# A one-word-per-row load of w1 moved from ScalarE's queue to SyncE's, between the first two x loads

## The chip, the cores and the metric

The kernel runs on one core of one Trainium2 chip. The metric is the device time of one execution in microseconds. Engines are named as in the profile: PE (TensorE matmuls), PEld (its weight loads), DVE (VectorE), ACT (ScalarE), POOL (GpSimd) and SP (SyncE). SyncE, ScalarE and GpSimd each have a DMA queue of their own; in the profile SyncE's transfers run on q1, ScalarE's on q10 and GpSimd's on q0.

## The reference

```python
# x: 16 x 256 x 512, w1: 512 x 4096, w2: 2048 x 512, all float32
h = x @ w1
gate, value = np.split(h, 2, axis=-1)
h = np.maximum(gate, 0) * value
return (h @ w2).astype(np.float32)
```

With the batch flattened x has 4096 rows.

## The kernel before

The kernel computes both products in float16 with a seven-product scheme for 2 x 2 blocks, so each pair of blocks needs seven matmul groups (P1 to P7) in place of eight, and sums of operands are made beforehand. Rows of x are worked in four sets of 1024; a set is two halves (A1, A2) of 512 rows. Hidden columns go in 16 blocks of 128. For each set a loop over the blocks makes the gated hidden values g (the class `Block`), and the second product (`mm2_stream`) of one set runs between the matmuls of the next. The order of all instructions on each engine is written out by hand: what the program issues first on an engine or a queue runs first there.

The start is special, since nothing is on the chip yet. In the order in which things are issued:

- VectorE clears a tile `warm`, and TensorE runs eight matmuls on it (`idle(NWARM)`, L177) whose results are not used.
- ScalarE's queue has one transfer, L172: `first`, a tile of 128 x 4 float32 into which one word of each of the 512 rows of w1 is loaded. A row of w1 is 4096 float32, so the words lie 16 KB apart. No instruction reads `first`. ScalarE's only other transfer is L335, one of the last stores of the output.
- SyncE's queue has the loads of the first set: two of x rows 0 to 511 into `xf` (L418, 256 rows each; the profile calls that buffer g_S, since `xf` lies in a tile of that name), two of w1 for hidden blocks 0 and 1 (L404, `fetch_wl(0, 0, 2)` the gate columns and `fetch_wl(0, 1, 2)` the value columns; the profile calls the buffer g), one of further x rows (L421), two of w1 for block 2 (L404), and one more of x (L424). SyncE's next transfer is L558, far later.
- GpSimd makes the identity matrices, waits with a small copy (L427) for the value columns of blocks 0 and 1, and then fetches the rest of w1 and w2 with a cast to float16 (L358, L362).
- TensorE transposes the x rows (`turn_pair`, L382) in two halves; ScalarE and VectorE copy them out of PSUM (L384). They also cast the loaded w1 to float16 (`cast_w`, L400), first of all the gate columns of block 0. Then come the first real matmuls (`Plain`, L255), which need the transposed x and the cast w1. Three blocks go in this plain way; the seven-product blocks (L205) follow.

The order of the start, in the code:

```python
idle(NWARM)
turn_pair(xo, 0, psw, "W")      # x rows 0 to 255
cast_w(0, 0)                    # gate columns of block 0
idle(NFILL)
turn_pair(xo, 2, psx, "X")      # x rows 256 to 511
whole[0].gates((0,))            # first real matmuls
```

The last stores go out at the end of `mm2_stream`: SyncE's L330 and L337, and L335 on ScalarE's queue.

Of the kernel before, what the change touches and what calls it, by code (L numbers as in the profile page):

```python
# [9 lines left out]
F32, F32R, F16 = dt.float32, dt.float32r, dt.float16  # L10
# [6 lines left out]
P = 128  # L17
# [12 lines left out]
@with_exitstack  # L30
def kernel(ctx: ExitStack, tc: tile.TileContext, x, w1, w2, out):

    nc = tc.nc
    x2 = x.flatten_outer_dims()
    out2 = out.flatten_outer_dims()  # L40
    flagpool = ctx.enter_context(tc.tile_pool(name="flagpool", bufs=1))
    flag = flagpool.tile([1, 1], dt.int32, name="flag")
    with ExitStack() as fast:
        unfit = fast_way(fast, tc, x2, w1, w2, out2, flag)
    with tc.If(unfit > 0, label="general"):
        with ExitStack() as general:
            general_way(general, tc, x2, w1, w2, out2)
# [52 lines left out]
def fast_way(ctx, tc, x2, w1, w2, out2, flag):  # L100

    nc = tc.nc
# [10 lines left out]
    wpool = ctx.enter_context(tc.tile_pool(name="wpool", bufs=1))  # L113
# [8 lines left out]
    w1_v = w1.rearrange("(e p) (g j) -> p e g j", p=P, g=2)  # L122
# [44 lines left out]
    nc.vector.memset(warm[:, 0, :HALF], 0.0)  # L167
    ident = {t: wpool.tile([P, P], t, name=f"ident{k}") for k, t in enumerate((F32, F16))}
    gate = wpool.tile([P, 1], F32, name="gate")

    first = wpool.tile([P, 4], F32, name="first")
    nc.scalar.dma_start(out=first[:128], in_=w1_v[:128, :, 0, 0])  # L172

    def idle(n):
        for _ in range(n):
# [14 lines left out]
    def look(t, at, of):  # L190
        sq = tmp.tile([P, 1024], F16, name="sq", tag="sq", bufs=1)
        sq = sq[:, :of] if len(t.shape) == 2 else sq[:, :of].rearrange("p (a b) -> p a b", a=t.shape[1])
        nc.scalar.activation(sq, t, SQUARE, scale=(P / of) ** 0.5, accum_out=st[:, at:at + 1])
# [208 lines left out]
    def fetch_wl(jb, g_, n=1):  # L402
        c, i = place[jb]
        nc.sync.dma_start(out=wl[c][:, :, g_, i * P:(i + n) * P], in_=w1_v[:, :, g_, jb * P:(jb + n) * P])  # L404
# [7 lines left out]
    def look_x(s, i):  # L412
        b = i // 2
        t = rows[s, b // 2][:, b % 2] if s else (xf, xh)[b // NB][:, b % NB]
        look(t[:, i % 2 * 256:i % 2 * 256 + 256], 4 * NB * s + i, 256)

    for b in (0, 2):
        nc.sync.dma_start(out=xf[:, b:b + 2], in_=x_v[0, :, b:b + 2])  # L418
    fetch_wl(0, 0, 2)
    fetch_wl(0, 1, 2)  # L420
    nc.sync.dma_start(out=xg[:, :2], in_=x_v[0, :, NB:NB + 2])  # L421
# [116 lines left out]
    for s in range(NS):  # L538
        if s:
            g, go = g_tiles()  # L540
        first = NPLAIN if s == 0 else 0
# [111 lines left out]
```

## Time and profile before

| | |
|---|---|
| median of 14 runs | 309.54 us (309.23 to 310.46) |
| the profiled execution: time | 309.09 us |
| its span in the profile | 307.3 us |
| PE busy in the span | 299.7 us (98%) |
| DVE, ACT, POOL busy | 219.3, 189.8, 139.9 us |
| granted clock of TensorE | 1.00 |
| issue of L172 (`first`) on ScalarE's queue | at 0.82 us, 476 ns; landed 4.2 us after |
| issues of L418 (x) on SyncE's queue | at 0.85 and 1.38 us; landed 4.4 and 5.0 us after |

Times in the profile count from the start of the span. An issue's duration is that of the issuing engine's instruction, not that of the transfer; a landing is when its semaphore told of it. The share of DMA in a window is the mean busy share of the core's 16 DMA engines; as it is counted by a packet's start, it can be over 1.

### The profile page before, as it was taken

To read this page: it belongs to the slowest core of one execution; us is meant where nothing else is said; L and a number is where in the kernel's file an instruction comes from. 1 tells how busy PE (TensorE), PEld (TensorE's weight loads), DVE (VectorE), ACT (ScalarE), POOL (GpSimd) and SP (SyncE) were. 2 spreads that over 40 slices of the span, in tenths; PEclk is the share of its full clock that TensorE was granted. 3 is DMA by queue.
4 is the path that set the end of the run, shared out by engine and by line. 5 is a ranking of instruction groups with operands and counts; after the bars stand their busy time and mean duration, and the time that the engine had idled before them with its cause. 6 is when DMAs were issued, how large, how long until landed. Compare 5 with 4: busy or idle time off the path is not lost.

```text
span 307.3 us, 5116 instructions
## 1 busy us (share of the span) xinstructions
PE 299.7 (98%) x1868; PEld 182.1 (59%) x1868; DVE 219.3 (71%) x346; ACT 189.8 (62%) x457; POOL 139.9 (46%) x127
## 2 busy tenths in 40 slices
PE   7999999999999999999999999999999999999994
PEld 3574444588844444488864444458884444448883
DVE  1798898896468888884338888885526888888401
ACT  2557776568577676737856767656857767673230
POOL 1749999810004438990002345994000433898000
PEclk9999999999999999999999999999999999999999
DMA  6999986989615740064130000037321100000223
GB/s 226 305 204 205 210 207 184 188 152 192 233 59 102 140 102 1 2 132 143 68 139 23 12 34 2 0 69 140 138 82 57 34 10 26 0 2 0 70 87 124
DMA packets 34410, 31.54 MB, mean 103 GB/s; under 512 B 14448, under 2 KB 28784, under 8 KB 34160
## 3 DMA queue, kind: packets, MB, share of 16 engines
q1 hardware_dynamic: 24608, 20.32, 22.0%
q0 software_dynamic: 9104, 10.75, 21.3%
q8 instruction: 15, 0.25, 0.3%
q10 hardware_dynamic: 672, 0.13, 0.2%
q14 instruction: 11, 0.09, 0.1%
HBM read 24.12 MB, written 11.53 MB: 116 GB/s over the span
## 4 chain that ended last, share of the span: by engine, by line
PE 95%; DMA 2%; ACT 0%; SPq 0%; issue 0%; ACTq 0%
PE Y L205 26%; PE X L205 17%; PE W L205 17%; PE Y L291 14%; PE X L291 9%; PE W L291 9%; DMA g<-in_w_dram 2%; PE W L255 2%; PE X L255 1%; PE Y L255 1%; SPq L418 0%; PE X L390 0%; ACT Y L212 0%; ACT wr L400 0%; ACT pv L333 0%
## 5 line engine op out<-in xcount | busy, mean ns | idle before, releaser
L280 POOL TENSOR_TENSOR g_S<-g 128x512 f16<-128x512 f16 (+1 forms) x46 | 58.2, 1294 | 126.1 <-DVE g L244 126.1
L205 PEld LDWEIGHTS <-wt 128*128 128x128 f16 x488 | 47.7, 98 | 55.8 <-issue 0.3
L205 PE MATMUL X<-x_A,wr 128*128 128x512 f16 x244 | 72.5, 379 | 0.1
L205 PE MATMUL Y<-x_S,wt 128*128 128x512 f16 x244 | 72.6, 379 | 0.0
L205 PEld LDWEIGHTS <-wr 128*128 128x128 f16 x366 | 35.8, 98 | 41.4 <-issue 0.4
L232 DVE SCALAR_TENSOR_TENSOR cc<-W,pu 128x512 f32<-128x512 f32 x61 | 42.2, 692 | 24.1 <-ACT pu L226 24.1
L212 ACT COPY Y<-X 128x512 f32<-128x512 f32 x61 | 34.8, 570 | 38.0 <-PE X L205 37.5
L291 PEld LDWEIGHTS <-g_S 128*128 128x128 f16 x512 | 50.1, 98 | 5.8
L238 DVE SCALAR_TENSOR_TENSOR cc<-Y,pu 128x512 f32<-128x512 f32 x61 | 42.2, 692 | 6.2
L226 ACT ACTIVATE pu<-Y 128x512 f32<-128x512 f32 x61 | 36.4, 596 | 13.8 <-PE Y L205 13.8
L233 DVE SCALAR_TENSOR_TENSOR g<-X,cc 128x512 f16<-128x512 f32 x61 | 42.2, 692 | 2.4
L244 DVE SCALAR_TENSOR_TENSOR g<-Y,cc 128x512 f16<-128x512 f32 x61 | 41.6, 681 | 1.8 <-PE Y L205 1.8
L291 PEld LDWEIGHTS <-g 128*128 128x128 f16 x384 | 37.5, 98 | 8.2
L219 ACT ACTIVATE pu<-W 128x512 f32<-128x512 f32 x61 | 36.7, 602 | 0.3 <-PE W L205 0.3
L205 PE MATMUL Y<-x_A,wt 128*128 128x512 f16 x122 | 36.3, 379 | 0.0
L205 PE MATMUL W<-x_S,wt 128*128 128x512 f16 x122 | 36.3, 379 | 0.0
L205 PE MATMUL W<-x_S,wr 128*128 128x512 f16 x122 | 36.3, 379 | 0.0
L291 PE MATMUL X<-w,g 128*128 128x256 f16 x256 | 31.2, 273 | 0.0
L291 PE MATMUL Y<-v,g_S 128*128 128x256 f16 x256 | 30.6, 273 | 0.0
L321 DVE SCALAR_TENSOR_TENSOR o<-W,pv 128x256 f32<-128x256 f32 x16 | 6.8, 424 | 29.5 <-PE W L291 29.5
L280 POOL TENSOR_TENSOR g_S<-g,g_S 128x512 f16<-128x512 f16 x18 | 21.8, 1210 | 1.4
L280 POOL TENSOR_TENSOR g_S<-g_S,g 128x512 f16<-128x512 f16 x18 | 20.8, 1157 | 1.4
(76 smaller groups left out, 284.4 us busy)
## 6 DMA issues: line engine op xcount, KB each, us to landing
out_dram<-pv SPq DMA_DIRECT2D x15, 256.0 KB, 2.0
out_dram<-o SPq DMA_DIRECT2D x13, 256.0 KB, 2.4
x<-in_x_dram POOLq DMA_DIRECT2D x3, 1024.0 KB, 9.4
xn<-x SPq DMA_DIRECT2D x12, 256.0 KB, 3.0
g_S<-in_x_dram SPq DMA_DIRECT2D x4, 512.0 KB, 6.4
wr<-in_w_dram POOLq DMA_DIRECT2D x4, 512.0 KB, 13.0
w<-in_w_dram POOLq DMA_DIRECT2D x4, 512.0 KB, 15.3
g<-in_w_dram SPq DMA_DIRECT2D x2, 512.0 KB, 6.5
```

Source lines behind the costliest of these rows:

```text
L205: nc.tensor.matmul(ps, W(wn, self.jb)[:, b], self.xo[xn][:, b, :], start=fresh and b == 0, stop=b == 1, skip_group_check=True)
L212: nc.scalar.copy(out=self.Y, in_=self.X)
L219: nc.scalar.activation(self.p5, self.W, COPY, scale=GS)
L226: nc.scalar.activation(self.u2, self.Y, COPY, scale=-GS)
L232: nc.vector.scalar_tensor_tensor(out=self.c12, in0=self.W, scalar=GS, in1=self.u2, op0=MULT, op1=ADD)
L233: nc.vector.scalar_tensor_tensor(out=self.g[:, self.jb, :TH], in0=self.X, scalar=0.0, in1=self.c12, op0=MAX, op1=MULT)
L238: nc.vector.scalar_tensor_tensor(out=self.c22, in0=self.Y, scalar=-GS, in1=self.p5, op0=MULT, op1=ADD)
L244: nc.vector.scalar_tensor_tensor(out=self.g[:, self.jb, TH:], in0=self.Y, scalar=0.0, in1=self.c22, op0=MAX, op1=MULT)
L255: nc.tensor.matmul(ps[:, ts], W(names[e // 2], self.jb)[:, e % 2], self.a[:, e, ts], start=e == 0, stop=e == 3, skip_group_check=True)
L280: eng.tensor_tensor(go[n][:, h0:h1], go[i0][:, h0:h1], go[i1][:, h0:h1], op=op)
L291: nc.tensor.matmul(ps, go[gn][:, k, b * P:(b + 1) * P], V[vn][:, k, :], start=fresh and k == 0, stop=k == NHC - 1, skip_group_check=True)
L321: nc.vector.scalar_tensor_tensor(out=d["o1"][:, HALF:], in0=d["W"], scalar=1 / GS, in1=d["pu"][:, 1], op0=MULT, op1=ADD)
```

## The change

The load of `first` is taken from ScalarE's queue and issued on SyncE's, after the first of the two x loads and before the second. Its tile is allocated there too. Source words, destination shape and everything else stay as they are.

```diff
-    first = wpool.tile([P, 4], F32, name="first")
-    nc.scalar.dma_start(out=first[:128], in_=w1_v[:128, :, 0, 0])
-
...
+    first = wpool.tile([P, 4], F32, name="first")
     for b in (0, 2):
         nc.sync.dma_start(out=xf[:, b:b + 2], in_=x_v[0, :, b:b + 2])
+        if b == 0:
+            nc.sync.dma_start(out=first, in_=w1_v[:, :, 0, 0])
     fetch_wl(0, 0, 2)
     fetch_wl(0, 1, 2)
     nc.sync.dma_start(out=xg[:, :2], in_=x_v[0, :, NB:NB + 2])
```

SyncE's queue then has, in order: x rows 0 to 255, `first`, x rows 256 to 511, the two loads of w1 for blocks 0 and 1, and the rest as before. ScalarE's queue has L335 alone. On the other engines the instructions and their order are the same.

## The prediction

> **What bounds the kernel now.** I read the page's busy times first, then the chain of waits, then the timeline and the windows of the first microseconds, because all that the change touches happens there, and last the timeline of the end, where the only other transfer on ScalarE's queue sits.
>
> The page, engines and the chain that ended last:
>
> ```profile
> PE 299.7 (98%) x1868; PEld 182.1 (59%) x1868; DVE 219.3 (71%) x346; ACT 189.8 (62%) x457; POOL 139.9 (46%) x127
> ...
> PE 95%; DMA 2%; ACT 0%; SPq 0%; issue 0%; ACTq 0%
> ```
>
> TensorE sets the time, 95% of the chain, and the other 2% are one transfer. Which one, the chain in order of time says (start, length, what), window 0 to 13 us:
>
> ```profile
> 0.85 0.47 SPq L418
> ...
> 1.38 0.53 SPq L418
> ...
> 1.95 5.97 DMA g<-in_w_dram
> ...
> 7.95 0.41 ACT wr L400
> ...
> 8.40 1.10 PE X L255 x8
> 9.51 0.86 PE Y L255 x4
> ```
>
> SyncE issues the two x loads (L418, I call them x0 and x1), then the first w1 load (L404, the gate columns of hidden blocks 0 and 1). That one lands at 7.92, ScalarE casts it, and from 8.40 TensorE goes on to the end with hardly a pause. So the landing at 7.92 is the number to follow: what moves it moves the end by as much, since casts, Pool's fetches behind L427 and all later work hang on the same stream of landings.
>
> Issues, from the timeline (start, length, queue and line):
>
> ```profile
> 0.82 0.48 ACTq L172 DMA_DIRECT2D first<-in_w_dram  x1
> 0.85 1.05 SPq L418 DMA_DIRECT2D g_S<-in_x_dram  x2
> ...
> 1.32 1.28 ACT L384 ACT_TABLE_LOAD   x1 [1.32 <-PEq L637]
> ...
> 5.41 1.06 PE L382 MATMUL W<-ident,g_S 128*128 128x128 f32 x8 [0.87 <-DMA g_S<-in_x_dram]
> ...
> 303.30 0.38 ACTq L335 DMA_DIRECT2D out_dram<-pv  x1
> ```
>
> And the windows of those stretches; the columns that matter are the last two, the busy share of the DMA engines and GB/s:
>
> ```profile
> 2.00:2.45 0.45, 0.45 (x2) 0.15 (x1) 0.00 (x0) 0.45 (x1) 0.00 (x0) 1.00 0.35 38
> 2.45:2.95 0.50, 0.50 (x2) 0.15 (x1) 0.00 (x0) 0.16 (x1) 0.00 (x0) 1.00 0.03 0
> 2.95:3.25 0.30, 0.30 (x2) 0.15 (x1) 0.00 (x0) 0.00 (x0) 0.00 (x0) 1.00 0.56 198
> 3.25:5.70 2.45, 1.58 (x7) 0.62 (x6) 0.00 (x0) 0.00 (x0) 0.00 (x0) 1.00 1.06 391
> 5.70:7.10 1.40, 1.40 (x15) 1.24 (x13) 0.69 (x1) 0.59 (x1) 0.00 (x0) 1.00 1.09 360
> ```
>
> Small packets start near 2.0 (by the DMA queues' counts 242 of the 528 packets that ScalarE's queue has in the first 10 us lie between 2 and 3 us, and 9 of SyncE's), then for half a microsecond nothing moves on either queue, then x0, x1 and w1 run back to back on full engines. From about 3 us on the DMA engines are the bound of the start.
>
> **The change, part by part.**
>
> *ScalarE's queue loses L172.* Its issue took 0.48 us before the table load at 1.32. ScalarE then stands idle 3.9 us for the first transposes (the wait of L384 for PE W), so an earlier table load gains nothing.
>
> *SyncE's queue gets it, after x0.* A second x issue took 525 ns, `first` 476 ns, so x1 and every SyncE issue behind it (four L404, L421, L424) goes out some 0.48 us later, plus a gap of 0.06. Is that seen? x0 is 512 KB; at 391 GB/s that is 1.34 us, so it moves from about 2.95 to 4.4, x1 to 5.7, the first w1 load to 7.1 (estimates; the landing is seen at 7.92). x0 needed 2.1 us from issue (0.85) to bulk movement (2.95), the longest such lag here; x1, issued at 1.9 instead of 1.38, would be ready at 4.0, 0.4 before its turn, the w1 load at 2.5 + 2.1 = 4.6, a whole 1.1 early. So the later issue costs nothing, the cover being x0's own transfer; if that cover goes, it costs 0.48. Behind them SyncE comes to L558, which waits 35.5 us in all for w2, so nothing later notices. Pool's L427 waits 7.6 us for the second w1 load and its weight fetches are queued behind it: they move with the landings, not on their own.
>
> *Engine time of `first`.* The trace gives its queue 2.9% of the 16 engines in the first 10 us: 0.29 us per engine. Of this 0.16 (0.35 x 0.45) ran at 2.00 to 2.45, when no x was ready, and 0.13 between x0's packets. Behind x0 in one queue all 0.29 stands before x1 and the w1 load: **+0.16**.
>
> *The half microsecond without movement.* 2.45 to 2.95 has a DMA share of 0.03. The trace does not say whose it is. If it belongs to `first` (half of its rows asked for, their words not yet back), it moves with `first` to behind x0, where x1 waits for it in the same queue; if it belongs to whatever comes first on the engines, x0 now meets it, and `first` adds nothing. Bounds: minus 1.0 us (x0 starts at 1.95, where `first` started, instead of 2.95, and `first` passes smoothly) to plus 0.50 (x0 still starts at 2.95 and the pause appears a second time). I take **+0.50**: x0 was issued only 0.03 us after `first`, yet the 9 x packets that moved before the pause were followed by none until 2.95, so x has a slow first access of its own, and 4-byte reads of 512 far-apart rows are the likelier ones to have theirs.
>
> *ScalarE's last store.* L335 (303.30, lands 2.3 us later, 305.6, the last landing) becomes the first transfer on that queue. In this trace the first issue on ScalarE's queue took 476 ns, the second 377; SyncE's first issue 471 against 330 for its last. So **+0.10** on the path that ends last. To the first packet `first` took 1.18 (0.82 to 2.00) and L335's packets some 0.87: upper bound +0.10 + 0.31 = 0.41; lower bound 0.
>
> *Sum.* 0 + 0.16 + 0.50 + 0.10 = +0.76 us. The profiled execution took 309.09 (span 307.30 and 1.79 around it), which would become 309.85; the median of the 14 runs, 309.54, lies 0.45 above it and becomes 310.30.
>
> **Two rules of the Trainium skill against these rows.** The rows first: L172 lasted 0.82 to 1.30 and the first L418 0.85 to 1.32, side by side, and the first L418 (471 ns) was shorter than the second (525), which had no rival. "Perfetto Trace Analysis", section "DMA Instruction — HWDGE", says that one descriptor generator is shared by the issuing sequencers and locked for one at a time. By that rule x0 stood behind `first`, and the new order would free it: the sum would be the faster rival's below. The rows show no lock in the issue times; what happens after them they leave open. "DMA: Bandwidth & Descriptors", section "Issuing engines are not separate DMA queues", says that all issuing engines end on the same 16 DMA engines and that the choice of issuer only saves issue time; by it the sum is the hidden 0.48, so 309.54. The pause on both queues at once agrees with shared engines; but within one queue x1 has to follow `first`, which the rule leaves out.
>
> **Rivals.**
>
> *Faster: x0 no longer waits for `first`.* Mechanism: at the start both queues feed the same engines, `first` got its packets in at 2.00 and x0's bulk only at 2.95. With x0 ahead it may start at 1.95 and everything behind it up to 1.0 earlier: -1.0 + 0.16 + 0.10 = -0.74, 308.80. For it: the pause lies between `first`'s two halves, and both resume together. Against it: the 9 x packets that came through before the pause were stopped as well. It decides as soon as x0's lead exceeds 0.26. PE could use it: x0's transposes wait 0.87 us for x at 5.41, and the warming matmuls end at 4.54.
>
> *No change: the pause is the start's own.* x0 meets the same 2.95, and `first` passes behind it at the pace of its packets: +0.16 and 0 to 0.10, or an x0 earlier by one or two tenths: -0.1 to +0.3, 309.7 as the middle. For it: the second half of `first` went through between x0's packets with the engines at 1.06 busy, so its rows needed no visible wait once the engines were running. This is the strongest argument against my +0.50.
>
> *Much slower: the later issue shows as well.* If the engines run dry behind x0 because `first`'s 512 descriptors hold the queue, x1's 0.48 is no longer covered: 0.16 + 0.50 + 0.48 + up to 0.41 = +1.55, 311.1. Against it: the 1.1 us in hand of the w1 load.
>
> *The change does nothing.* `first` is never read by any instruction, so no wait is tied to it; only its place counts. That is the second rival with all terms at zero.
>
> **How the numbers follow.** A measurement of this kernel can tell about 0.2%, 0.6 us, from no change. Forecast (pause behind x0) 0.40; much slower 0.12; no change 0.24; faster 0.24. Of the forecast's 0.40 about 0.04 falls below +0.6, because part of the pause may be hidden under x0's last packets; of the faster case 0.02 stays within 0.6. So slower 0.36 + 0.12 = 0.48, same 0.24 + 0.04 + 0.02 = 0.30, faster 0.22. As the cases of both signs hold most of the chance: the forecast's own range is 309.9 to 310.7 (pause 0.1 to 0.5, tail 0 to 0.41). The range that should hold 8 in 10 reaches from the faster case's near half (308.9) to short of the much slower one (310.9).
>
> **What would show it.** In the profile after: the L404 landing now at 7.92 should come at about 8.6 and TensorE's first L255 at about 9.1; a stretch of low DMA share of up to 0.5 us should stand between x0 and x1 near 4.4 to 5; L418's second issue at 1.9; L335's issue near 0.48 us long. If instead x0's bulk starts before 2.6 the faster rival is right; if the landing is within 0.3 of 7.92 the pause is the start's own. If the landing is the same and the end later, it is ScalarE's queue. I am wrong altogether if TensorE shows new pauses after 10 us.

## The result, and the profile after

The changed kernel takes 312.07 us (median of 10 runs, 311.10 to 313.73), the kernel before 309.69 (47 runs): a ratio of 1.0078 [1.0066, 1.0091], 2.38 us slower. Two more executions of it, the profiled one among them, took 310.97 and 310.38 and are not in that median. A second measurement gave 311.88 against 309.88, 1.0053 [1.0031, 1.0075]. The forecast was +0.76 us. The sign is right; the size is a third of what came, and the time lies outside the range of 308.9 to 310.9.

The profiled execution took 310.97 us, with a span of 309.1 (before: 309.09 and 307.3). The lines between `first`'s old place and its new one have moved up: what was L404 is now L401, the casts are L397, the first real matmuls L252; the x loads are L416 and `first` is L418.

The page, engines and the chain that ended last:

```profile
PE 299.6 (97%) x1868; PEld 182.0 (59%) x1868; DVE 219.2 (71%) x346; ACT 189.7 (61%) x457; POOL 139.6 (45%) x127
...
PE 95%; DMA 2%; SPq 0%; ACT 0%; issue 0%
```

TensorE has the same work (299.6 against 299.7 us) in a longer span: the time went into waiting. The chain in order of time, window 0 to 15 us (start, length, what), says where:

```profile
0.85 0.47 SPq L416
...
1.38 0.46 SPq L418
...
1.88 0.51 SPq L416
...
2.43 7.06 DMA g<-in_w_dram
...
9.51 0.41 ACT wr L397
...
9.97 1.10 PE X L252 x8
```

The issues stand as forecast: `first` at 1.38, the second x load (x1) at 1.88, the first w1 load at 2.43. But that load lands 7.06 us after its issue and not 5.97, at 9.49 instead of 7.92. The cast follows it, and the first real matmuls start at 9.97 instead of 8.40: **1.57 us**, from a later landing alone.

In between, from the timeline (start, length, queue and line; in brackets the wait before it), and the longest waits of TensorE in the first 15 us:

```profile
1.38 0.46 SPq L418 DMA_DIRECT2D first<-in_w_dram  x1
...
4.38 1.06 PE L379 MATMUL W<-ident,g_S 128*128 128x128 f32 x8
...
8.00 1.09 PE L379 MATMUL X<-ident,g_S 128*128 128x128 f32 x8 [2.34 <-DMA g_S<-in_x_dram]
```

```profile
PE X L379 <- DMA g_S<-in_x_dram: 2.3, 1, 2.3
...
PE X L252 <- ACT wr L397: 0.9, 1, 0.9
```

The first x load (x0) is there *earlier* than before: its transposes start at 4.38 instead of 5.41, without a wait. The second, behind `first`, is 1.48 us *later*: 8.00 instead of 6.52. The 0.87 us wait for x0 of the profile before has become a wait of 2.3 us for x1.

The windows of those microseconds (busy time and count of PE, PEld, DVE, ACT, POOL; granted clock; busy share of the DMA engines; GB/s):

```profile
2.00:2.45 0.45, 0.45 (x2) 0.15 (x1) 0.00 (x0) 0.10 (x1) 0.00 (x0) 1.00 0.83 209
2.45:2.95 0.50, 0.50 (x2) 0.15 (x1) 0.00 (x0) 0.00 (x0) 0.00 (x0) 1.00 0.94 291
...
3.25:5.70 2.45, 2.41 (x13) 1.22 (x11) 0.65 (x1) 0.22 (x1) 0.00 (x0) 1.00 0.97 217
5.70:7.10 1.40, 0.00 (x0) 0.00 (x0) 0.04 (x1) 0.37 (x1) 0.00 (x0) 1.00 0.77 257
7.10:9.50 2.40, 1.09 (x8) 0.86 (x8) 0.00 (x0) 0.00 (x0) 0.00 (x0) 1.00 1.03 349
```

The stretch without movement (0.03 and 0 GB/s before, 2.45 to 2.95) is gone: 291 GB/s flow there, x0's. But from 3.25 to 7.10, where before 391 and 360 GB/s flowed, it is 217 and 257. Note the share: 0.97 and 0.77. The engines are *not* idle for most of it, they are occupied by packets that take long. In the trace, 2048-byte packets of x last up to 1.2 us, where 84 ns is usual; 30 of those recorded in the first 10 us last over 0.2 us, in the trace before none. Looking for a pause in the share, as the prediction proposed, finds none (from 2 us on no quarter of a microsecond is below about 0.4); the bytes show it. In quarters of a microsecond from 0 to 10 us, first the kernel before, then the changed one:

```profile
GB/s 0 0 0 0 0 0 0 0 2 67 0 8 230 361 394 361 369 394 402 418 418 410 385 369 381 336 348 360 340 352 348 340 352 360 352 373 377 385 385 393
```

```profile
GB/s 0 0 0 0 0 0 0 33 164 279 213 377 401 393 233 54 197 181 164 205 262 270 193 152 180 283 319 352 316 356 299 311 307 328 385 393 389 393 397 397
```

Before: late, but then full at once. After: a full microsecond earlier, and then three microseconds (the fifteenth to the twenty-sixth number, 3.5 to 6.5 us) at about half.

The profile's sum: +1.57 at the first matmuls, -0.29 at 163.35 us, where TensorE of the kernel before has a short gap that the changed one lacks, +0.48 behind ScalarE's last ACTIVATE (4.90 us from its start to the end of the span instead of 4.42). That is +1.76, and the span grew by 1.8. The median grew by more; in over half of the runs the clock takes something too, and that is experiment 7.

### The profile page after: what moved, and what is told of

Its sections match the earlier page's. It is cut to its first block, busy times and chain, and to the rows that moved or that the text cites. A ratio compares the mean times of both kernels' runs of the same rounds, so it can differ in the third digit from the quotient of the medians.

```text
span 309.1 us, 5116 instructions
## 1 busy us (share of the span) xinstructions
PE 299.6 (97%) x1868; PEld 182.0 (59%) x1868; DVE 219.2 (71%) x346; ACT 189.7 (61%) x457; POOL 139.6 (45%) x127
## 4 chain that ended last, share of the span: by engine, by line
PE 95%; DMA 2%; SPq 0%; ACT 0%; issue 0%
PE Y L202 26%; PE X L202 17%; PE W L202 17%; PE Y L288 14%; PE X L288 9%; PE W L288 9%; DMA g<-in_w_dram 2%; PE W L252 2%; PE X L252 1%; PE Y L252 1%; SPq L416 0%; PE X L387 0%; SPq L418 0%; ACT wr L397 0%; ACT pv L330 0%
```

## The experiments

After the result I held that *something in `first` itself* breaks the flow behind x0, and the rivals were: its 512 far-apart rows, the number or the size of its pieces, its bare presence between the two x loads, x1's later issue, the queue. Edits are against the changed kernel unless another is named. "Cast" is the start of the first w1 cast in the profiled run: 7.95 before, 9.51 after.

### 1. Without `first`, and with it at the very front

```diff
 e1_no_first, e15_no_first5:
-        if b == 0:
-            nc.sync.dma_start(out=first, in_=w1_v[:, :, 0, 0])
 e2_sp_front:
+    nc.sync.dma_start(out=first, in_=w1_v[:, :, 0, 0])
     for b in (0, 2):
```

> This leaves `first` out (no instruction reads it, the result is the same). Theory A (the 512 far-apart reads of `first` disturb the x and w1 transfers that follow them on each DMA engine): with no such reads x0 starts near 2.0 us as in the changed kernel, nothing stalls behind it, the first w1 load is seen at about 6.7 to 7.0 us and the time is 0.9 to 1.2 us below before, about 308.6. Theory B (w1 or the start itself has a first-access pause that somebody must pay, and `first` pays it): the stretch of half-busy DMA engines stays, between x1 and the first w1 load or inside it, the first w1 load is seen at 8.5 to 9.5 us and the time is 310.5 to 312. Theory C (512 small packets in SyncE's queue are the cost): like A, 308.6.

> `first` on SyncE's queue, ahead of both x loads. Theory A: its disturbance falls where nothing else moves, as before; x0 starts near 3 us, is issued 0.5 us later than before, full rate from then on; first w1 load seen at 7.9 to 8.4, time within +0.5 us of before (309.6 to 310.2). Theory B: the same. Theory C: 512 small packets in SyncE's queue cost what they cost in the changed kernel, first w1 load at 9.0 to 9.5, time 311 to 312.

> Without `first`, again, on the chip of the next run: median within 0.3 us of before, every run's granted clock from 0.995. If the first result (309.56) was that chip's luck: 310 to 310.5 with some low-clock runs.

Without it: 309.56 against 309.51, ratio 0.9995 [0.9984, 1.0007], and on another chip 309.35 against 309.88, 0.9982 [0.9971, 0.9994]. Cast at 8.20 and 8.03. None of the three theories had that time. At the front of SyncE's queue: 310.56, 1.0038 [1.0020, 1.0056], cast at 9.10, between the forecasts; there x0 itself stands behind `first`, the flow falls to 66 GB/s at 4.25 us, and x0 lands at 5.82 instead of 4.25 in the changed kernel. The GB/s line of the kernel without `first` (e1):

```profile
GB/s 0 0 0 0 0 0 0 25 164 188 352 377 426 393 393 401 401 410 385 238 283 193 205 258 299 324 352 320 332 369 377 385 414 385 410 393 395 371 363 346
```

x0 starts as early as in the changed kernel, so its earlier start comes from `first` no longer being ahead of it on ScalarE's queue. And here, too, the flow sinks later (193 to 299 GB/s at 4.75 to 6.25 us), but less deeply and less long. An early start is partly lost again even with no small transfer about; that is why it is worth nothing here (cast at 8.20, 8.03 and, in e13 of experiment 5, 7.89, where the kernel before has 7.95).

### 2. Is it w1's far-apart rows?

```diff
 e3_sp_x_words:
-            nc.sync.dma_start(out=first, in_=w1_v[:, :, 0, 0])
+            nc.sync.dma_start(out=first, in_=x_v[0, :, 0, ::P])
```

> As the changed kernel, in the same place in SyncE's queue, with the same 512 words of 4 bytes, but read from rows of x that the load before it has just read (512 bytes apart) and not from the rows of w1; w1 is then not touched early. Theory A: no stall behind it, first w1 load seen near 7.0 to 7.3, time 308.7 to 309.2. Theory B: as without `first`, the pause is paid by the w1 load, 310.5 to 312. Theory C: as the changed kernel, x1 lands at 7.5 to 8, first w1 load at 9.0 to 9.5, time 311 to 312.

512 words out of the rows that x0 has just read: 310.86, 1.0055 [1.0030, 1.0080], cast at 9.07. The rows of w1 are not the cause.

### 3. Is it the number of pieces, or their size?

```diff
 e6_sp_128:
+            nc.sync.dma_start(out=first[:, :1], in_=w1_v[:, 0, 0, :1])
 e9_sp_16:
+            nc.sync.dma_start(out=first[:16, :], in_=w1_v[:16, 0, 0, :4])
 e10_sp_wide (tile 128 x 64):
+            nc.sync.dma_start(out=first, in_=w1_v[:, 0, 0, :64])
```

> As the changed kernel, but `first` has one word of each of 128 rows of w1, 128 packets in place of 512. Per-packet theory: the stall behind it shrinks to a quarter, some 0.3 us, x1 is complete near 5.6 us, the first cast of w1 starts near 8.3 to 8.6, time 309.6 to 310.1. Per-transfer theory (any small transfer in the queue breaks its flow once): as the changed kernel, first cast at 9.0 to 9.6, time 310.9 to 312.1.

> As the changed kernel, but `first` is 16 pieces of 16 bytes (one for each DMA engine) of 16 rows of w1. If any transfer put between x0 and x1 in SyncE's queue breaks the flow behind it: x1's packets come at half rate for over a microsecond, first cast at 9 or later, time 310.5 to 311.5, as with 128 words (310.7). If the small packets in number make the stall: nothing to see, x1 at full rate, first cast near 8.2 as without `first`, time within 0.3 us of before.

> As the changed kernel, but `first` is 128 pieces of 256 bytes, as many packets as the run with 128 words, of the same 128 rows of w1, each 64 times as long. If the smallness (4-byte writes) makes the stall: milder than with 128 words, 309.6 to 310.1. If the number of packets or the far-apart rows make it: as with 128 words, 310.4 to 311.

| between x0 and x1 | time (us) | ratio | cast |
|---|---|---|---|
| 512 pieces of 4 bytes (the change) | 312.07 | 1.0078 [1.0066, 1.0091] | 9.51 |
| 128 pieces of 4 bytes | 310.72 | 1.0030 [1.0004, 1.0056] | 9.10 |
| 16 pieces of 16 bytes | 311.05 | 1.0041 [1.0021, 1.0062] | 9.72 |
| 128 pieces of 256 bytes | 311.16 | 1.0057 [1.0041, 1.0074] | 8.77 |

The GB/s line with 16 pieces:

```profile
GB/s 0 0 0 0 0 0 0 25 156 270 328 401 401 401 116 90 115 90 188 221 205 217 299 315 356 410 307 340 340 336 340 336 328 332 344 373 381 402 397 395
```

256 bytes in 16 pieces are enough for the break: about 100 GB/s from 3.5 to 4.5 us, and the cast no earlier than in the changed kernel. My theory that `first`'s own engine time or its many descriptors do it falls. What all of these have in common is *a* transfer between x0 and x1 on SyncE's queue.

### 4. Is it the moment, or the queue?

```diff
 e4_act_late, e12_act_late5 (against the kernel before):
+    nc.scalar.copy(out=gate, in_=warm[:, 0, :1])
     nc.scalar.dma_start(out=first[:128], in_=w1_v[:128, :, 0, 0])
```

> `first` on ScalarE's queue as before, but issued behind the table load and a one-column copy, near 2.4 us in place of 0.8, so that its packets come near 3.3 us, when x0 is moving. Theory A: the stall moves with it although the queue is another: x0 starts near 2.0, then half-busy engines for 2 to 3 us, first w1 load at 8.5 to 9.5, time 310.5 to 312. Theory B: the same as A. Theory C (only SyncE's queue matters): no stall, first w1 load near 7.0, time 308.6 to 309.2.

> The kernel of the run with `first` on ScalarE's queue behind the first x load, again and with more rounds, since its median lay 0.3 us below before. If that was real: 309.1 to 309.4 where before has 309.5, ratio 0.9985 to 0.9995 with an interval below 1. If it was chance: ratio 0.9995 to 1.0005.

The issue did not wait for the copy, but it came at 1.26 us, behind x0's 0.85 and just ahead of x1's, so the order in time is that of the change and the queue is another. (x1, which no longer has to be issued behind it on SyncE, goes out at 1.38 instead of 1.88; that difference comes with the queue.) 309.23, 0.9990 [0.9978, 1.0002]; again 309.51, 0.9986 [0.9972, 1.0001]. Cast at 8.32 and 8.29. The GB/s line of the first of them:

```profile
GB/s 0 0 0 0 0 0 0 25 131 213 270 385 418 393 272 68 190 296 361 394 385 287 283 295 295 315 336 369 369 365 369 381 397 373 377 397 389 385 385 340
```

The hole has the same depth (68 GB/s at 3.75 us, the changed kernel has 54 there), but a quarter of a microsecond later 190 and then 296 to 394 flow. In the second profile the flow does not go below 200 there. The same words, issued in the same tenth of a microsecond or so between the same transfers, cost 2.0 to 2.4 us on SyncE's queue (0.4 of it at the end, experiment 6) and nothing on ScalarE's. By the Trainium skill ("DMA: Bandwidth & Descriptors", section "Issuing engines are not separate DMA queues") the choice of issuer saves only issue time; the measurement decides against it here, with the reserve that x1's issue moved too.

### 5. Moving x1 instead

```diff
 e11_x1_on_act:
-        nc.sync.dma_start(out=xf[:, b:b + 2], in_=x_v[0, :, b:b + 2])
+        (nc.scalar if b else nc.sync).dma_start(out=xf[:, b:b + 2], in_=x_v[0, :, b:b + 2])
 e13_x1_late (and `first` left out):
+    nc.gpsimd.memset(xf[:, 2:4, :320], 0.0)
```

> As the changed kernel with `first` behind x0 on SyncE's queue, but the second x load (x1) goes out on ScalarE's queue at 0.8 us and so does not stand behind `first`. Queue theory: x0 and x1 run side by side, `first` passes beside x1, the w1 load behind it starts when x1 ends; no long idle of TensorE between the two transposes, first cast 7.9 to 8.6, time 309.2 to 310.2. Shared-engine theory (small packets slow whatever runs on the engines then): half rate as in the changed kernel, first cast at 9 or later, 311 to 312.

> No `first` at all, but the second x load (x1) waits for a GpSimd memset of part of its buffer, so that it is issued near 1.9 to 2.0 us as in the changed kernel, with nothing between x0 and x1 in the queue. Issue theory (x1's later issue is what costs; the cover I named does not hold): x1's packets stall as in the changed kernel, first cast at 9 or later, time 310.5 to 312. Transfer theory (the extra transfer in the queue is what costs): as without `first`, first cast near 8.2, 309.4 to 309.8.

With x1 on ScalarE's queue (issued at 0.82, `first` still behind x0 on SyncE's): 311.16, 1.0054 [1.0039, 1.0068], but the six runs fall into two groups, 309.5 to 309.7 (two runs, the profiled one among them: cast at 7.91, no long break) and 310.9 to 311.7 (four). All six had a mean granted clock of 0.996 or more, which leaves out a halving as in experiment 7, but not the slow start that e17's profile shows in experiment 6. No trace of the slower group exists, and it stays open. The kernel before has such runs too: measured beside e13, 6 of its 32 runs took 311.03 to 311.27, at clocks of 0.996 to 1.0.

The second was to put x1's issue half a microsecond later with nothing in between. It missed: the memset took only 0.63 us, from 0.82, so x1 was issued at 1.48 and the first w1 load at 1.90. Its 309.90, 0.9997 [0.9980, 1.0014], therefore says nothing on the later issue.

### 6. A transfer in both places, and one at the end

```diff
 e14_both_places (against the kernel before):
         nc.sync.dma_start(out=xf[:, b:b + 2], in_=x_v[0, :, b:b + 2])
+        if b == 0:
+            nc.sync.dma_start(out=again, in_=w1_v[:16, 0, 0, :4])
 e7_sp_after_x1:
-        if b == 0:
+        if b == 2:
 e8_sp_last: `first` behind the last of SyncE's early loads
 e17_tail_only (against the kernel before):
+    nc.sync.dma_start(out=again, in_=w1_v[:16, 0, 0, :4])   # behind the last early load
```

> The kernel before with `first` early on ScalarE's queue, and besides 16 pieces of 16 bytes between x0 and x1 on SyncE's queue. Shield theory (the early load takes the slow first accesses on itself, what follows runs smoothly): no stall, first cast 7.95 to 8.2, time 309.4 to 310. If the in-between transfer hurts in any case: stall behind it, first cast near 9, time 310.3 to 311.3.

> `first` one place later, between the second x load and the first w1 load. Queue theory (what stands behind the 512 small packets in the same queue loses about 1.2 us, wherever they stand): x1 is complete near 5.3 us as without `first`, the first w1 load stretches instead; first cast at 9.0 to 9.6; time 310.5 to 312 with fewer low-clock runs, since x1's transposes come at 6.3. Start theory (the stall belongs to the chip's first microseconds, not to the place in the queue): stall again near 4 us or none; first cast near 8.2, time 309.4 to 309.8.

> `first` at the end of SyncE's first loads, behind the last x load. Queue theory: nothing that matters stands behind it, so like the kernel without `first`: first cast near 8.2, time 309.3 to 309.7. Shared-engine theory (512 small packets cost the 16 engines the same wherever they run): 0.2 to 0.5 us later, 309.8 to 310.1.

> The kernel before with one more transfer (16 pieces of 16 bytes, read by nobody) at the end of SyncE's first loads, where no load that the start needs stands behind it. If one more transfer on SyncE lengthens the end by itself: first cast within 0.15 us of 7.95, SyncE's last drain 0.38 us later than its turn, time 0.3 to 0.6 us above before. If the longer end belongs to the stall or to the early load's new place: no change, within 0.15 us of before.

With the early load left on ScalarE's queue and 16 pieces more between x0 and x1: no break. x1 was issued at 1.95, the cast starts at 8.05 and the first real matmuls at 8.51 (before: 7.95, 8.40). Its GB/s line:

```profile
GB/s 0 0 0 0 0 0 0 0 2 51 0 25 181 246 378 378 394 386 354 410 426 410 393 361 393 365 348 356 340 344 365 340 348 356 344 377 360 377 401 385
```

So neither the transfer in between nor x1's later issue breaks the flow where `first` goes ahead on ScalarE's queue and x0 starts late. The landing of x1 tells the cases apart. It is 7.28 to 8.40 in all eight profiles that have a transfer between x0 and x1 on SyncE's queue and nothing ahead on ScalarE's, and 5.55 to 5.87 in the five where x0 starts as early and nothing stands between the two (e1, e15, e13, e7, e8). With `first` on ScalarE's queue at that moment it is 6.52 and 6.14 (experiment 4), and 6.52 here. The late landing of x1 comes with both: an x0 that starts at 2.0 *and* that transfer on its own queue. In the eight profiles x1 is also issued at 1.88 to 2.10, in the five at 1.38 to 1.48; no run separates this later issue from the transfer.

This kernel is nevertheless slower, 310.54, 1.0020 [1.0003, 1.0037], and in its profile nearly the whole loss is at the end: 5.63 us from ScalarE's last ACTIVATE to the end of the span, where the kernel before has 4.42. With the extra transfer behind all early loads (e17) the end is like it, 5.51 us, at 310.68, 1.0028 [1.0019, 1.0038]. Two things stand there. Here is what SyncE does on the program's last line (engine, operation and count: shortest, median and longest in ns, first and last start), in the kernel before, the changed one, and e17:

```profile
L648 SPq DRAIN  x3: 7/13/35, 306.4 to 307.0; - x3
```

```profile
L648 SPq DRAIN  x3: 7/13/131, 307.8 to 308.5; - x3
```

```profile
L650 SPq DRAIN  x3: 7/13/130, 308.3 to 309.0; - x3
```

The second of the three drains takes 0.13 us instead of 0.007 and starts 0.38 us behind the first instead of 0.07, and the span ends 1.31 us after the first drain instead of 0.88: 0.43 us later. That is so in all 13 profiles of kernels with one more transfer on SyncE's queue than before, and in none of the 7 with the old number. Most of the rest of these two kernels' loss at the end, about 0.6 us, is the order of SyncE's eight last waits: where the store that lands last is waited for first, the other seven waits (some 0.08 us each) follow it instead of preceding it.

The profiled run of e17, 311.48, loses 1.2 us at the start besides, and not by a landing: its first w1 cast is at 8.12, but the first real matmuls come only at 9.26.

```profile
5.57 1.94 PE L383 MATMUL W<-ident,g_S 128*128 128x128 f32 x8 [0.70 <-DMA g_S<-in_x_dram]
...
9.26 0.60 PE L256 MATMUL X<-x_A,wr 128*128 128x256 f16 x4
```

The eight transposes take 1.94 us where the kernel before needs 1.06, and the next eight 1.69 instead of 1.04, although the windows give a granted clock of 1.00 there. The trace's first record of the clock is at 9.06 us (at 4.07 in the kernel before; over the 20 profiles at 3.96 to 9.38), so such a slow start is in no run's granted clock. It is not of the change: the profiles of kernels with and without `first` have it.

Behind x1 (e7): 310.56, 1.0033 [1.0002, 1.0065]; its profiled run, with the cast at 7.97, was the fastest of ten (309.42), and two of the others took 313.5. Behind all (e8): 310.04, 1.0017 [0.9997, 1.0037], with the longer drain. Its profiled run, 313.19, had the cast at 9.87. There `first` is issued only at 9.30, behind a slow stretch (119 to 283 GB/s from 4.75 to 6.5 us), so up to then it is a kernel without `first`: an early start can end in a late landing without a transfer in between, only more seldom. Eight of e8's ten runs lie at 309.5 to 310.8. Without any `first`, none of 22 runs (e1, e15) is over 310.2 and none of e13's ten over 310.72.

### 7. Why the median is over the profile: the clock

```diff
 e5_after_fill, e18_after_fill5:
-NFILL = 1
+NFILL = 11
 e16_after: the changed kernel again, without an edit
```

> The changed kernel beside the others: 311.5 to 312.3, in two groups, near 311.1 with a clock from 0.996 and near 312.7 with a clock up to 0.994.

> The changed kernel with 11 in place of 1 unused matmuls between the two x transposes (about 2.2 us of TensorE at full clock), so that TensorE is not idle there. Clock theory: in the changed kernel the runs with a mean granted clock up to 0.993 take about 312.7 us and those from 0.998 about 311.1; with the pause filled the slow ones go, the granted clock is 0.995 to 1.0 in every run and the median 310.9 to 311.3, the highest below 312. Transfers-only theory (the start's transfers alone scatter the time): nothing changes, median 311.8 to 312.3, highest over 313.

> The changed kernel with the 10 more unused matmuls, again. Clock theory: no run with a granted clock below 0.995, all runs between 310.8 and 312.3, where the changed kernel had 310.5 to 314.5 with 4 of 7 runs at 0.993 or less. If the filling does nothing for the clock: runs of 313 and more, with clocks of 0.987 to 0.993, come back.

The repeated kernel gave the ratio told above, and its profiled run, 314.51 us, holds the answer. The windows (columns as before; the seventh figure is the granted clock):

```profile
4.60:8.01 3.41, 1.17 (x10) 0.78 (x8) 0.69 (x1) 0.58 (x1) 0.00 (x0) 0.97 0.90 260
8.01:11.50 3.49, 2.62 (x12) 2.04 (x13) 1.09 (x3) 1.12 (x3) 0.00 (x0) 0.50 1.07 364
11.50:14.84 3.34, 3.34 (x12) 1.57 (x11) 1.19 (x3) 0.79 (x3) 2.93 (x4) 0.54 1.08 278
14.84:20.00 5.16, 4.92 (x39) 2.91 (x38) 3.69 (x7) 2.49 (x6) 5.16 (x8) 1.00 1.30 173
```

and TensorE's first work in it:

```profile
8.45 1.97 PE L379 MATMUL X<-ident,g_S 128*128 128x128 f32 x8 [2.68 <-DMA g_S<-in_x_dram]
10.84 1.89 PE L252 MATMUL X<-x_A,wr 128*128 128x256 f16 x8 [0.43 <-ACT wr L397]
```

TensorE waits 2.68 us for x1, has little to do until then, and from 7.77 to 14.60 it is granted half its clock (the edges are the clock's own records; the windows above are cut 0.24 us later): the eight matmuls of L252 take 1.89 us, which in the other profile take 1.10. Its lag behind the kernel before grows from 2.44 us at the first L252 to 4.57 at 17.4 us. So the landing costs twice: once as a wait, and once more as a halved clock that the wait brings on. The half clock lasts 6.83 us, twice 3.41; that agrees with the window of about 3.4 us that the Trainium skill gives in "TensorE: Matmul & The Clock Gate", section "Part 1: The HAM clock gate (the "warmup" mystery)", which also says that the window runs free. By that, whether an idle stretch of some 3 us costs anything depends on where it falls. The profiles agree: in the 3.41 us before the halving (4.36 to 7.77) TensorE was busy for 1.41 us, and in e8, whose clock is halved from 11.50 to 14.91, for 1.18 us in the stretch before. The changed kernel's first profile, with 1.64 and 1.97 us busy in its first two such stretches (from 4.02 and 7.43), kept its clock.

The runs agree. Of the 19 timed or profiled runs of the changed kernel in both measurements, 11 had a mean granted clock of 0.994 or less and took 312.65 us on average; 8 had 0.995 or more and took 310.98, 1.67 less. Not all of that need be the clock: between the two profiles the halved clock adds 2.13 us (2.44 to 4.57), but the slower one's first w1 load also lands 0.87 us later (10.36 against 9.49). The kernels of experiments 2 and 3 have such runs too (3 of 10, 2 of 10, 1 of 6 and 1 of 4, at 312.09 to 314.42 us). None of the 123 runs of the kernel before whose clock is on record, and none without a transfer added to SyncE's queue, was below 0.995.

With ten more matmuls between the two halves of the transposes, TensorE does not rest while x1 comes: 311.50 (four runs) and 311.35 (six), 1.0058 [1.0039, 1.0076] and 1.0048 [1.0031, 1.0065], clocks 0.996 to 1.0 in all ten, and none over 312.11, where the changed kernel reaches 314.51. The loss by the clock is gone, but the fill itself puts x1's transposes from 8.00 to 8.60 and 8.88, so the median falls by only half a microsecond.

## Why the prediction was wrong, step by step

- **Later issues of SyncE (0).** They came where they were put (x1 at 1.88, forecast 1.9). With the early load present, an x1 issued at 1.95 moved the first matmuls by 0.11 (e14). In the changed kernel the cover that I named, x0's transfer, is thinner, since x0 starts earlier; the later issue alone could not be tried there (e13 missed).
- **Engine time of `first` (+0.16).** Not seen as such. Sixteen pieces, with a thirty-second of the descriptors, have the same cast time as 512.
- **The half microsecond without movement (+0.50): the step that failed.** The pause did belong to `first` on ScalarE's queue, or most of it; without that, x0 moves at 2.0 and lands about a microsecond earlier (at 4.13 to 4.55 in the kernels where no load goes out ahead of x0 or with it, at 5.27 in the kernel before). So the bound that I gave, x0 at 1.95, was right, and so was the other, that a pause appears behind x0. I took them for alternatives. Both happened, and the second is not a pause of 0.5 but three microseconds at half speed: x0 1.03 us earlier, x1 1.48 later, the first w1 landing 1.57 later, where my sum had +0.66 (0.16 + 0.50). I had priced the break by the length of the only hole that the trace before had, on engines that were still empty; here x1's packets, up to 1.2 us long, hold the engines.
- **ScalarE's last store (+0.10).** The row for it, L332, has an issue of 0.38 us as before, and no later landing: 0. But the end did grow by 0.48, of which 0.43 come with SyncE's drain. I had looked at the queue that loses a transfer, and not at what the queue that gains one has to do at the end.
- **The clock: missing.** Eleven of nineteen runs at 1.67 us are 0.97 us on the mean, an upper bound, since a later landing may be part of it. The prediction said that TensorE would follow the landing one to one; it did not ask how long TensorE would stand idle and what an idle stretch does.

Sum as it came, in the profile: 1.57 - 0.29 + 0.48 = 1.76 of span; and the median, which holds the clock's part, 2.38.

**The rivals.** The faster one's mechanism was real, and the mark that I set for it ("if x0's bulk starts before 2.6 the faster rival is right") was met, with the opposite result: what counts is not x0 but the last of the three landings. Without any `first`, where only that mechanism is left, the time is the same within 0.2% (0.9995, 0.9982). "No change" falls by the ratio. The much slower one, +1.55, has the place right (the engines behind x0), but not the reason: 512 descriptors are not needed, 16 pieces do it, and the engines stayed busy (0.97 and 0.77). That its sum, which holds up to 0.41 for the end, is nearly the 1.57 of the landing alone is luck. The marks of 8.6 for the landing and 9.1 for the first matmuls were missed by 0.9 each; the low share was not to be seen, as the loss was in GB/s at a full share; and after 10 us TensorE showed no new pauses but, in more than half of the runs, a lower clock.

**The rules.** The locked generator of "Perfetto Trace Analysis", section "DMA Instruction — HWDGE", would have made x0's earlier start a gain; x0 did start earlier, with issue times as before (0.85, 0.47 us long), and nothing here shows whether the lock is the reason.

**What stays open.** Why a transfer behind an early-started x0 makes x1's packets slow on the same queue and much less on another; why SyncE's second drain comes 0.38 us behind the first with one transfer more; whether x1's issue, half a microsecond later, has a part in it; what the slower group of e11 is, and that of the kernel before; and why an early start sometimes ends in a late landing with nothing in between, as in e8's profile.

No version is clearly faster than the kernel before. Without `first` the ratios are 0.9982 [0.9971, 0.9994] and 0.9995 [0.9984, 1.0007], with `first` behind x0 on ScalarE's queue 0.9986 and 0.9990; only the first of the four intervals excludes 1, and all lie within the 0.2% that a measurement can tell.

## What to carry to other kernels

Follow the landing that the first real work waits for, not that of the first transfer: a start that begins earlier can end later, and only GB/s, not the engines' busy share, shows it. Price a small transfer that is slipped between large ones on one queue by the large one that comes behind it, and look at both ends of that queue, its last drains and waits too. When a wait of TensorE grows to two or three microseconds, ask what it does to the granted clock, and compare the clocks of the runs, since one profile may have missed it. For the first microseconds look at how long equal matmuls take as well: a granted clock of 1.00 can stand beside matmuls at half speed.

## What was not expected of the hardware

- 16 pieces of 16 bytes between two loads of 512 KB on one queue brought the flow from 401 GB/s down to about 100 for a microsecond, with x1 landing at 7.35 instead of 5.62 us in the kernel without any.
- The same 512 words on another queue at nearly the same moment: no loss of time (0.9990, 0.9986).
- At the start of the program, reads that begin a microsecond earlier sink to about half speed later on: for three microseconds in the changed kernel, and for one and a half even without any small transfer (193 to 299 GB/s at 4.75 to 6.25 us).
- One transfer more on SyncE's queue, wherever it stands: the end of the program 0.43 us later, 13 of 13 profiles; and up to 0.6 us more where the store that lands last is the first that SyncE waits for.
- A clock halved for 3.41 or 6.83 us after a stretch of 3.41 us in which TensorE was busy for 1.18 and 1.41 us, and not after 1.64 us (experiment 7).
